# A hybrid decoder layer: its late matrix products computed as eight plain block products in place of seven combined ones

## The chip, the cores and the metric

The kernel runs on one core of one Trainium2 chip, in one launch. The metric is the device time of that launch in microseconds (us). The kernel before takes 2474.23 us, the median of three runs (2469.93 to 2477.15). TensorE does the matrix products. VectorE (DVE), ScalarE (ACT) and GpSimd (POOL) do elementwise work, and every DMA here is issued from the SyncE (SP) queue. Matrix products collect their sums in PSUM, eight banks of 128x512 float32.

## The reference, cut to what matters

SEQ and D_MODEL are 1024, D_FF is 2816, there is one layer and one batch entry.

```
h = rmsnorm(x)
proj = h @ w_in                        # 1024 x 12312: inputs of three mixers, and three gates
y_gla, y_mlstm, y_fox = gla(proj), mlstm(proj), fox(proj)    # each 1024 x 1024
merged = sum over n of (ys[n] @ w_branch[n]) * sigmoid(gates[n] + b_gate[n])
x = x + merged @ w_out
h = rmsnorm(x)
a, g = split(causal_dwconv(h @ w_up))  # 2 x 2816 columns
x = x + (silu(g) * a) @ w_down         # 2816 -> 1024
out = rmsnorm(x)
```

The change touches the three branch products, the product with `w_out` (each 1024x1024x1024) and the product with `w_down` (1024x2816x1024). It leaves the products with `w_in` and `w_up` as they are.

## The kernel before, in words

**Precision.** Operands are float32. Each is split into a high and a low part of type float32r (`split`, L166: ACT casts to get the high part, DVE subtracts to get the low one). A block product is three matmuls: high by high, high by low, low by high. A matmul here has 128x128 weights and a 128x512 moving tile.

**Seven products.** Every large product is cut into 2x2 blocks and computed with seven block products in place of eight (Strassen's scheme in Winograd's form), numbered 1 to 7. For one `Job` (256 output rows by 1024 columns) each of the seven is 4 blocks of depth times 3 matmuls, so 12 matmuls, which the text calls a step. The scheme needs sums of blocks on both sides: of the weights (`prep`, L1157, by POOL at L1168), of the moving side (`combos`, L1035, by POOL or DVE at L1059 to L1069), and of the results (`compute`, L1188, with ACT copies at L1199 and DVE adds at L1090, L1114, L1264, L1276, L1344).

**Order of the work.** `gemms` (L1239) walks one list of steps and prepares the weights of two steps ahead of the one it computes (AHEAD = 2). The list of the first part holds 48 jobs of `w_in` (336 steps), then three branch products of 4 jobs each, then the product with `w_out`, 4 jobs. Beside it `mixers` (L1482) yields small steps of the mLSTM, GLA and FoX mixers in that order. The loop at L1498 takes one mixer step per list step; from list step NX = 110 on it takes a second one in every fourth (RATE = 4). When the mixers are done, the loop of `w_in` runs on alone to its end.

**The moving side.** It lives in seven groups of SBUF of 16 KB per partition (`group`, L152). `put` (L256) splits a 128x512 block into one. When a step is computed, functions hung on it (`after`) call `more`, which loads and prepares the next product's blocks into groups as they come free. The branch products read the mixers' outputs from DRAM (`y_d`), the last reads `w_dn`.

**Merging and the two ends.** `merge_job` (L1079) multiplies a branch result by its gate and adds it to `mg`, two groups; that add is POOL's (L1095). `out_job` (L1101) splits `mg` as its weights and adds the result to x. `row_norm` and `blocks0`, `blocks1` then normalise and transpose the rows for `w_up`. The down product runs in three chunks of depth (8, 8 and 6 blocks); after each step DVE adds the PSUM bank to rows `acc` in SBUF (L1344), and `finish` (L1354) does the final norm of a row and stores it.

**Scheduling.** The instructions of each engine stand in an order that the framework's scheduler fixes at build time from the order of the program text, its own estimate of durations, and free buffers. At run time every engine works its list strictly in that order, except that weight loads of TensorE overlap matmuls.

Of the kernel before, what the change touches and what calls it, by code (L numbers as in the profile page):

```python
# [36 lines left out]
MAP_FF = {1: 3, 2: 4, 5: 0, 6: 1, 3: 2, 7: 5, 4: 6}  # L37
# [4 lines left out]
ROLL_DN = (3, 4, 0, 1, 2, 5, 6)  # L42
DN_CHUNKS = (8, 8, 6)


class Job:
# [3 lines left out]
    def __init__(self, src1, src2, xc, post, name, nk=4, done=None, wide=False, acc=None, load=None, kept=None):  # L50
        self.src, self.xc, self.post, self.name, self.nk = (src1, src2), xc, post, name, nk
        self.done, self.wide, self.acc, self.load = done, wide, acc, load
        self.kept = kept
        self.raw, self.w, self.after = None, {}, {}
        self.second, self.held, self.inplace, self.sum1 = False, None, False, None

# [44 lines left out]
class Kern:  # L101
# [933 lines left out]
    def combos(self, n, block, xc, base, order, ytile, ttile, engs):  # L1035


        nc = self.nc
        ts = [None] * n
        due = []  # L1040

        def load(kh, i, hf):
            t = ytile()
            nc.sync.dma_start(out=t, in_=block(kh, i, hf))
            return t

        for p in order:
            for i in range(n):
                if p == 1:
                    src = load(0, i, 0)  # L1050
                elif p == 2:
                    src = load(1, i, 0)
                elif p == 3:
                    src = load(1, i, 1)
                elif p == 5:
                    b = load(0, i, 0)
                    src = ts[i] = ttile(i)
                    nc.sync.dma_start(out=src, in_=block(0, i, 1))
                    engs[p].tensor_tensor(out=src, in0=src, in1=b, op=ALU.subtract)  # L1059
                elif p == 6:  # L1060
                    b = load(1, i, 1)
                    src = ts[i]
                    engs[p].tensor_tensor(out=src, in0=b, in1=src, op=ALU.subtract)
                elif p == 7:
                    src = load(0, i, 0)
                    engs[p].tensor_tensor(out=src, in0=ts[i], in1=src, op=ALU.subtract)  # L1066
                else:
                    src = load(1, i, 0)
                    engs[p].tensor_tensor(out=src, in0=src, in1=ts[i], op=ALU.subtract)  # L1069
                due.append((p, i, src))  # L1070
                if len(due) > LAG:
                    q, m, t = due.pop(0)
                    self.put(xc, q, m, t, base)
                yield
        while due:
            q, m, t = due.pop(0)
            self.put(xc, q, m, t, base)

    def merge_job(self, env, n, b, p, xc):  # L1079
        nc, a = self.nc, self.a  # L1080

        def post(m, hf, x, y):
            pool, mg = env["late"], env["mg"]
            j = 2 * p + m
            sl = slice(512 * (1 - hf), 512 * (1 - hf) + 512)
            th = pool.tile([P, 512], F32, tag="gth", name="gth", bufs=2)
            nc.sync.dma_start(out=th, in_=self.g_d[8 * b + j][:, sl])
            if y is not None:
                t = x if (m, hf) == (1, 1) else y
                nc.vector.tensor_tensor(out=t, in0=x, in1=y, op=ALU.add)  # L1090
                x = t
            o = mg[j // 4][:, j % 4, sl]
            nc.vector.scalar_tensor_tensor(out=th if n else o, in0=th, scalar=1.0, in1=x, op0=ALU.add, op1=ALU.mult)
            if n:
                nc.gpsimd.tensor_tensor(out=o, in0=o, in1=th, op=ALU.add)  # L1095

        def kept(nm):
            return env["late"].tile([P, 512], F32, tag="s5", name=nm, bufs=4) if nm == "s5" else None
        return Job(a["w_br"][8 * b + 2 * p], a["w_br"][8 * b + 2 * p + 1], xc, post, "br", wide=True, kept=kept)

    def out_job(self, env, p, xc, rows, done):  # L1101

        nc = self.nc

        def load(job):
            mg = env["mg"]
            for i in range(2):
                rows[2 * p + i] = r = self.raw_tile(job, "x2")
                nc.sync.dma_start(out=r, in_=self.a["x"][(2 * p + i) * P:(2 * p + i + 1) * P, :])
            return [mg[kh][:, :, (2 * p + i) * P:(2 * p + i + 1) * P] for i in range(2) for kh in range(2)]  # L1110

        def acc(m, hf, b):
            o = rows[2 * p + m][:, 512 * hf:512 * hf + 512]
            nc.vector.scalar_tensor_tensor(out=o, in0=b, scalar=0.5, in1=o, op0=ALU.mult, op1=ALU.add)  # L1114
        return Job(None, None, xc, None, "wo", wide=True, acc=acc, load=load, done=lambda: done(p))

# [27 lines left out]
    def load_w(self, job):  # L1144
        if job.load is not None:
            job.raw = job.load(job)
            return
# [40 lines left out]
    def compute(self, job, p):  # L1188
        nc, post, acc = self.nc, job.post, job.acc
# [21 lines left out]
        if acc is not None:  # L1211
            if p == 1 or p == 2:
                acc(0, 0, b)
            elif p == 6 or p == 3:
                acc(0, 1, b)
            elif p == 5 or p == 7:
                acc(1, 1, b)
            elif p == 4:
                acc(1, 0, b)
        elif p == 1:  # L1220
# [18 lines left out]
    def gemms(self, seq):  # L1239
        due = []  # L1240
        while True:
            while len(due) <= AHEAD:
                nxt = next(seq, None)
                if nxt is None:
                    break
                job, p = nxt
                if job.raw is None:
                    self.load_w(job)
                self.prep(job, p)
                due.append(nxt)  # L1250
            if not due:
                return
            self.compute(*due.pop(0))
# [84 lines left out]
    def down_job(self, p, k0, nk, acc, wait, xc):  # L1338
        nc = self.nc

        def add(m, hf, b):
            def run():
                o = acc[2 * p + m][:, 512 * hf:512 * hf + 512]
                nc.vector.tensor_tensor(out=o, in0=o, in1=b, op=ALU.add)  # L1344
            if 2 * p + m in acc:
                run()
            else:
                assert hf == 0 and m == 0
                wait.append(run)
        src = [self.f_d[k0:k0 + nk, :, (2 * p + m) * P:(2 * p + m + 1) * P].rearrange("j p t -> p j t")  # L1350
               for m in range(2)]
        return Job(src[0], src[1], xc, None, "dn", nk=nk // 2, wide=True, acc=add)

    def finish(self, pool, x, tt, nfin):  # L1354
        nc = self.nc
        junk = self.swp.tile([P, D], BF16, tag="ws", name="junk", bufs=3)
        sm = pool.tile([P, 3], F32, tag="fsm", name="fsm", bufs=3)
        nc.scalar.activation(junk, x, AF.Square, accum_out=sm[:, 0:1])  # L1358
        self.rsqrt(sm[:, 2:3], sm[:, 0:1], 1.0 / D, sm[:, 1:2], 1)
        nc.vector.scalar_tensor_tensor(out=x, in0=x, scalar=sm[:, 2:3], in1=nfin, op0=ALU.mult, op1=ALU.mult)  # L1360
        nc.sync.dma_start(out=self.a["out"][tt * P:(tt + 1) * P, :], in_=x)
# [4 lines left out]
RATE = 4  # L1366
# [6 lines left out]
def body(tc, stop=None, **a):  # L1373
# [6 lines left out]
    with ExitStack() as ctx:  # L1380
# [10 lines left out]
        V, G = nc.vector, nc.gpsimd  # L1391

        def ytile():
            return env["cmb"].tile([P, 512], F32, tag="yb", name="yb", bufs=4)

        def ttile(i):
            return env["cmb"].tile([P, 512], F32, tag=f"T{i}", name="T")

        def wide(jobs):
            for p, j in enumerate(jobs):  # L1400
                j.second, j.inplace = p > 1, True
            return jobs

        def branch_blocks(b):
            return lambda kh, i, hf: k.y_d[b, 4 * kh + i][:, 512 * (1 - hf):512 * (1 - hf) + 512]

        def dn_blocks(k0, nk):
            return lambda kh, i, hf: a["w_dn"][k0 + kh * (nk // 2) + i][:, 512 * hf:512 * hf + 512]

        def out_blocks(kh, i, hf):  # L1410
            return a["w_out"][4 * kh + i][:, 512 * hf:512 * hf + 512]

        ready = []

        def sequence():
# [4 lines left out]
            for n, b in enumerate(order):  # L1420
                x = {}
                jobs = wide([k.merge_job(env, n, b, p, x) for p in range(4)])
# [363 lines left out]
```

## Time and profile before

| what | value |
|---|---|
| median of 3 runs | 2474.23 us |
| time of the profiled execution | 2473.26 us |
| its span, first to last instruction | 2471.3 us |
| TensorE matmul busy | 2318.3 us (94%), 11035 matmuls |
| VectorE busy | 1899.1 us (77%) |
| ScalarE busy | 1243.4 us (50%) |
| GpSimd busy | 1029.3 us (42%) |
| mean granted clock of TensorE | 0.977 of full speed |

A row of the profile names the line of the kernel, the engine, the operation and what it writes and reads ("x<-yb" writes tile x from tile yb). PE is TensorE. A granted clock of 1.00 is 2.4 GHz; the other level is half of it, so 0.90 over a stretch means that it ran a fifth of it at half speed. Busy time of TensorE is taken from modelled ends, so gaps between the starts of matmuls say more than it does. Stretches of the execution are named by their times from the span's start: the mixers mLSTM (to about 640 us), GLA (to 931) and FoX (to 1368) beside the products with `w_in`; the end of these at 1423.1; branches and `w_out` to 1771.4; the way into `w_up` to 1830.3; `w_up` to 2225.7; down to 2463.3.

### The profile page before, as it was taken

The page shows a single profiled execution, that of the slowest core. Times are in us where ns is not written, and L with a number is a line of the kernel's source. Part 1 is how long each engine was busy: PE and PEld are TensorE (multiplying, and loading weights), DVE is VectorE, ACT ScalarE, POOL GpSimd, SP SyncE. Part 2 cuts the span into 40 slices and gives each one's busy share as a digit, 9 for nine tenths or more (in the row PEclk, how much of TensorE's full clock was granted, in tenths as well). Part 3 has the DMA queues.
Part 4 walks back from the last instruction along what each step waited for, and adds up shares of the span by engine and source line. Part 5 has one row for each costly group of instructions (what it writes and reads, how often), then busy time and mean ns, then how long its engine had stood idle before and what let it go on. Part 6 is the DMA issues. An engine that isn't in the chain of part 4 may idle for free. (4 is left out here: it accounts for less than half of the span.)

```text
span 2471.3 us, 33215 instructions
## 1 busy us (share of the span) xinstructions
PE 2318.3 (94%) x11035; PEld 1905.4 (77%) x11035; DVE 1899.1 (77%) x3124; ACT 1243.4 (50%) x2441; POOL 1029.3 (42%) x972
## 2 busy tenths in 40 slices
PE   6999999988998999999999899888989999988898
PEld 5877778777777888888888787677868888866687
DVE  7687557676576766777776689988788898989986
ACT  5345455555566655555555554342555555553433
POOL 6222144444344443222222453577344443445662
PEclk8999999999999999999999999999999999999999
DMA  3355444554433435343333665553232332244631
GB/s 134 112 172 170 135 139 148 175 175 151 142 126 130 145 120 164 122 132 127 126 128 108 219 204 184 200 180 102 103 101 78 97 99 85 94 141 146 207 120 69
DMA packets 191500, 340.50 MB, mean 138 GB/s; under 512 B 17961, under 2 KB 80201, under 8 KB 190817
## 3 DMA queue, kind: packets, MB, share of 16 engines
q1 hardware_dynamic: 191328, 338.38, 41.9%
q8 instruction: 87, 1.43, 0.2%
q14 instruction: 85, 0.69, 0.1%
HBM read 242.73 MB, written 95.58 MB: 137 GB/s over the span
## 5 line engine op out<-in xcount | busy, mean ns | idle before, releaser
L160 PE MATMUL pg<-x,w6h 128*128 128x512 f32 x776 | 249.2, 401 | 18.1 <-DVE x L168 9.5
L160 PE MATMUL pg<-x,w4h 128*128 128x512 f32 x776 | 248.4, 401 | 13.5 <-DVE u L1264 9.2
L160 PE MATMUL pg<-x,w7h 128*128 128x512 f32 x776 | 247.2, 400 | 5.2 <-ACT u L1199 5.2
L160 PE MATMUL pg<-x,w1h 128*128 128x512 f32 x776 | 244.8, 396 | 3.7 <-ACT w1h L167 3.4
L160 PEld LDWEIGHTS pg<-x,w6h 128*128 128x128 f32 x776 | 146.1, 192 | 52.7 <-DVE x L168 13.2
L1168 POOL TENSOR_TENSOR sum<-up_raw 128x512 f32<-128x512 f32 x44 | 91.0, 2067 | 225.2 <-DMA up_raw<-in_w_up 203.0
L160 PEld LDWEIGHTS pg<-x,w4h 128*128 128x128 f32 x776 | 147.3, 193 | 46.1 <-DVE u L1264 6.4
L160 PEld LDWEIGHTS pg<-x,w7h 128*128 128x128 f32 x776 | 147.3, 193 | 36.3 <-ACT u L1199 6.0
L160 PEld LDWEIGHTS pg<-x,w1h 128*128 128x128 f32 x776 | 146.2, 191 | 34.6 <-ACT w1h L167 3.8
L160 PE MATMUL pg<-x,w7l 128*128 128x512 f32 x388 | 155.3, 400 | 12.8 <-DVE w7l L168 12.8
L160 PE MATMUL pg<-x,w4l 128*128 128x512 f32 x388 | 155.5, 401 | 7.6 <-DVE w4l L168 7.6
L160 PE MATMUL pg<-x,w1l 128*128 128x512 f32 x388 | 153.6, 396 | 6.9 <-DVE w1l L168 6.9
L160 PE MATMUL pg<-x,w6l 128*128 128x512 f32 x388 | 154.3, 398 | 0.1
L168 DVE TENSOR_TENSOR x<-yb,x 128x512 fp32r<-128x512 f32 x135 | 136.4, 1044 | 5.9 <-ACT x L167 4.8
L1313 DVE SCALAR_TENSOR_TENSOR c<-u,cols,c 128x1022 f32<-128x1022 f32 x84 | 126.7, 1508 | 15.5 <-ACT c L1309 15.5
L168 DVE TENSOR_TENSOR w5l<-sum,w5h 128x512 fp32r<-128x512 f32 (+1 forms) x98 | 99.0, 1010 | 37.8 <-ACT w5h L167 32.5
L160 PE MATMUL pa<-x,w3h 128*128 128x512 f32 x392 | 123.3, 394 | 1.7 <-DVE x L168 1.7
L160 PE MATMUL pa<-x,w5h 128*128 128x512 f32 x392 | 124.2, 398 | 0.8 <-DVE acc L1344 0.4
L160 PE MATMUL pg<-x,w5h 128*128 128x512 f32 x384 | 123.7, 402 | 0.9 <-DVE x L168 0.7
L160 PE MATMUL pg<-x,w2h 128*128 128x512 f32 x384 | 122.7, 399 | 1.6 <-POOL x L168 1.6
L160 PE MATMUL pg<-x,w3h 128*128 128x512 f32 x384 | 121.8, 398 | 0.0
L167 ACT CAST w5h<-sum 128x512 fp32r<-128x512 f32 (+1 forms) x98 | 60.2, 615 | 122.0 <-PE pg L160 86.9
(476 smaller groups left out, 6692.2 us busy)
## 6 DMA issues: line engine op xcount, KB each, us to landing
up_raw<-in_w_up SPq DMA_DIRECT2D x44, 512.0 KB, 3.8
yb<-y_d SPq DMA_DIRECT2D x84, 256.0 KB, 3.1
yb<-in_w_dn SPq DMA_DIRECT2D x77, 256.0 KB, 3.5
gate_raw<-in_w_in SPq DMA_DIRECT2D x24, 512.0 KB, 3.7
g_d<-st SPq DMA_DIRECT2D x48, 256.0 KB, 2.1
br_raw<-in_w_br SPq DMA_DIRECT2D x24, 512.0 KB, 4.8
gth<-g_d SPq DMA_DIRECT2D x48, 256.0 KB, 2.9
f_d<-c SPq DMA_DIRECT2D x22, 512.0 KB, 2.9
```

The source lines that it names most:

```text
L160: self.nc.tensor.matmul(out, lhsT=lhsT, rhs=rhs, start=start, stop=stop, skip_group_check=skip)
L167: self.nc.scalar.copy(out=hi, in_=src)
L168: (eng or self.nc.vector).tensor_tensor(out=lo, in0=src, in1=hi.bitcast(F32), op=ALU.subtract)
L1168: self.nc.gpsimd.tensor_tensor(out=t, in0=a, in1=b, op=op)
L1313: nc.vector.scalar_tensor_tensor(out=c[:, s:], in0=u[:, :T - s], scalar=self.col("fw", 44 * tap + m), in1=c[:, s:], op0=ALU.mult, op1=ALU.add)
```

## The change

The four products of the branches and `w_out` and the down product become plain products: eight block products, no block sums. A result stays in two PSUM banks over the whole depth. The products with `w_in` and `w_up` keep the seven.

- `Row` is 128 output rows by 1024 columns in four steps of 12 matmuls. It uses one high weight block for four matmuls (high and low of both halves of the columns), then its low block for two. The gate and merge of a branch read the two banks once per row; the add into `mg` moves from POOL to DVE.
- `Down` computes four rows of 128 at once, in eight banks, over all 22 blocks of depth, twice. It reads the activations `f_d` as weights, 256 KB at a time through two buffers, and keeps 14 of the 22 split blocks of `w_dn` in the seven groups, two to a group; the second half takes the kept ones first.
- `finish` adds the two banks of a row to x, in halves, and does the norm.
- The loads of a moving block are one per block; `yb` has six buffers.
- RATE becomes 10, and in FoX a second mixer step is taken in three of five list steps.
- The group of each step of `w_up` changes (`MAP_FF`); its step 3 is now in group 0, into which the first two blocks of `w_dn` go. Rows of `w_out` are normalised one by one as they get ready.

```diff
-MAP_FF = {1: 3, 2: 4, 5: 0, 6: 1, 3: 2, 7: 5, 4: 6}
+MAP_FF = {1: 1, 2: 2, 5: 3, 6: 4, 3: 0, 7: 5, 4: 6}
-DN_CHUNKS = (8, 8, 6)
+KEEP = 14
-RATE = 4
+RATE = 10
+class Row:
+    def prep(self, k, q):
+        if q % 2 == 0:
+            self.w[q // 2] = k.wsplit(self.raw[q // 2], "wo")
+    def compute(self, k, q):
+        if q == 0:
+            self.banks = (k.pg(), k.pa())
+        for i in range(2):
+            ...
+            x = [self.xc[q][2 * i + hf] for hf in range(2)]
+            first, last = q == 0 and i == 0, q == 3 and i == 1
+            for b, (xh, xl) in zip(self.banks, x):
+                k.mm(b, wh[:, ks], xh, first, False, True)
+                k.mm(b, wh[:, ks], xl, False, False, True)
+            for b, (xh, xl) in zip(self.banks, x):
+                k.mm(b, wl[:, ks], xh, False, last, True)
+        if q == 3:
+            for hf in range(2):
+                self.post(hf, self.banks[hf])
+class Down:
+    def steps(self):
+        n = len(self.order)
+        return [("r", r, 0) for r in range(4)] + [("k", i) for i in range(2, n - 2)] + [("r", r, n - 2) for r in range(4)]
...
 merge_row:
+                th = env["late"].tile([P, 512], F32, tag="gth", name="gth", bufs=4)
+                nc.sync.dma_start(out=th, in_=k.g_d[8 * order[n] + r][:, sl])
+                o = env["mg"][r // 4][:, r % 4, sl]
+                nc.vector.scalar_tensor_tensor(out=th if n else o, in0=th, scalar=1.0, in1=b, op0=ALU.add,
+                                               op1=ALU.mult)
+                if n:
+                    nc.vector.tensor_tensor(out=o, in0=o, in1=th, op=ALU.add)
...
 makes:
+                    m = dn["n"] = dn.get("n", -1) + 1
+                    g = m // 2 % 7
+                    if m % 2 == 0:
+                        dn["t"] = k.group(g, F32R, "xd")
...
+                    raw = k.dnp.tile([P, T], F32, tag="dr", name="dn_raw", bufs=2)
+                    nc.sync.dma_start(out=raw, in_=a["w_dn"][j])
...
 mixers' loop:
-                if n >= NX and n % RATE == RATE - 1:
+                if n % 5 in (0, 2, 4) if fox else n >= NX and n % RATE == RATE - 1:
                     next(mix, None)
...
 finish:
+        x = pool.tile([P, D], F32, tag="xr", name="xr", bufs=3)
+        nc.sync.dma_start(out=x, in_=self.x2_d[tt])
+        for hf, b in enumerate(banks):
+            o = x[:, 512 * hf:512 * hf + 512]
+            nc.vector.tensor_tensor(out=o, in0=b, in1=o, op=ALU.add)
+            nc.scalar.activation(junk[:, 512 * hf:512 * hf + 512], o, AF.Square, accum_out=sm[:, 2 + hf:3 + hf])
```

## Rows read from the trace of the kernel before

**Rows 1.** By stretch: us; PE, PEld, DVE, ACT, POOL busy (count); clock; DMA; GB/s
```profile
331.30:456.50 125.20, 115.86 (x616) 98.56 (x615) 86.60 (x166) 69.69 (x167) 62.72 (x76) 0.99 0.54 171
456.50:640.00 183.50, 167.03 (x902) 143.99 (x901) 125.16 (x259) 100.15 (x248) 77.84 (x93) 0.96 0.49 154
640.00:931.00 291.00, 273.06 (x1410) 226.38 (x1410) 200.72 (x468) 175.90 (x424) 129.42 (x204) 0.98 0.42 136
931.00:1368.00 437.00, 429.91 (x2313) 362.20 (x2312) 304.62 (x831) 234.62 (x492) 117.16 (x183) 1.00 0.39 127
...
1396.90:1423.10 26.20, 19.54 (x74) 15.33 (x73) 19.87 (x21) 13.95 (x24) 15.82 (x11) 0.87 0.67 219
1423.10:1771.40 348.30, 322.11 (x1378) 260.73 (x1377) 306.01 (x373) 149.46 (x268) 190.84 (x125) 0.97 0.50 169
1771.40:1830.30 58.90, 48.23 (x201) 37.27 (x200) 48.70 (x59) 31.18 (x53) 31.84 (x21) 0.91 0.20 70
1830.30:2201.00 370.70, 369.96 (x1633) 306.01 (x1631) 330.73 (x316) 191.23 (x279) 151.24 (x77) 1.00 0.29 94
2201.00:2225.70 24.70, 15.47 (x51) 11.85 (x50) 18.25 (x15) 11.67 (x19) 18.33 (x12) 0.80 0.60 198
2225.70:2340.70 115.00, 95.89 (x386) 75.30 (x385) 108.05 (x118) 43.91 (x75) 67.26 (x42) 0.92 0.57 185
2340.70:2463.30 122.60, 122.60 (x541) 101.09 (x539) 99.81 (x135) 46.13 (x84) 59.52 (x46) 1.00 0.28 91
```

**Rows 2.** Matmuls in order of time at full clock: start us, duration, instruction
```profile
1380.80 0.61 PE L160 MATMUL pg<-x,w2h 128*128 128x512 f32 x2
1381.25 0.39 PE L160 MATMUL pg<-x,w2l 128*128 128x512 f32 x1
1381.48 0.61 PE L160 MATMUL pg<-x,w2h 128*128 128x512 f32 x2
```

**Rows 3.** The same view behind a wait: the clock is at its lower level
```profile
1401.74 1.22 PE L160 MATMUL pg<-x,w7h 128*128 128x512 f32 x2 [4.46 <-ACT u L1199]
...
1403.19 1.05 PE L160 MATMUL pg<-x,w7h 128*128 128x512 f32 x2
1404.04 0.63 PE L160 MATMUL pg<-x,w7l 128*128 128x512 f32 x1
```

**Rows 4.** TensorE's waits, 1423.1 to 1771.4: total us, times, longest
```profile
PE pg L160 <- DVE w7l L168: 7.7, 3, 5.1
```

**Rows 5.** TensorE's waits, 2201.0 to 2225.7
```profile
PE pg L160 <- DVE u L1264: 9.2, 2, 5.9
```

**Rows 6.** VectorE's and GpSimd's groups, 1423.1 to 1771.4: count, busy us, mean ns
```profile
L168 DVE TENSOR_TENSOR x<-yb,x 128x512 fp32r<-128x512 f32 x71 | 70.3, 1028 | 2.4 <-ACT x L167 2.2
L1095 POOL TENSOR_TENSOR mg<-mg,gth 128x512 f32<-128x512 f32 x32 | 52.1, 1627 | 59.1 <-DVE gth L1093 46.3 <-PE pa L160 12.8
...
L168 DVE TENSOR_TENSOR x<-b,x 128x512 fp32r<-128x512 f32 x8 | 5.1, 686 | 0.0
```

**Rows 7.** TensorE's matmuls on tile x alone: us, busy (count), clock, DMA, GB/s
```profile
331.30:456.50 125.20, 86.45 (x362) 0.99 0.54 171
456.50:640.00 183.50, 117.90 (x480) 0.96 0.49 154
640.00:931.00 291.00, 212.18 (x842) 0.98 0.42 136
931.00:1368.00 437.00, 292.41 (x1193) 1.00 0.39 127
```

**Rows 8.** DMA issues: size, median us from issue to landing
```profile
yb<-y_d SPq DMA_DIRECT2D x84, 256.0 KB, 3.1
g_d<-st SPq DMA_DIRECT2D x48, 256.0 KB, 2.1
```

**Rows 9.** The end: VectorE's last instructions in order of time
```profile
2463.45 0.69 DVE L1344 TENSOR_TENSOR acc<-acc,pg 128x512 f32<-128x512 f32 x1
...
2466.34 1.28 DVE L1360 SCALAR_TENSOR_TENSOR acc<-acc,fsm,nfin 128x1024 f32<-128x1024 f32 x1 [0.73 <-POOL fsm L173]
```

More of the change, by code (lines that the diff above doesn't have):

```diff
@@ L1033, in fox @@
                 yield
[L1035 to L1115, printed above, removed]
@@ L1188, in compute @@
     def compute(self, job, p):
[L1189 removed]
+        nc, post = self.nc, job.post
         x = job.xc[p]
@@ L1246, in gemms @@
                 job, p = nxt
-                if job.raw is None:
-                    self.load_w(job)
-                self.prep(job, p)
+                if isinstance(job, (Row, Down)):
+                    if job.raw is None:
+                        job.load(self)
+                    job.prep(self, p)
+                else:
+                    if job.raw is None:
+                        self.load_w(job)
+                    self.prep(job, p)
                 due.append(nxt)
@@ L1252, in gemms @@
                 return
-            self.compute(*due.pop(0))
+            job, p = due.pop(0)
+            if isinstance(job, (Row, Down)):
+                job.compute(self, p)
+            else:
+                self.compute(job, p)
             yield
@@ L1336, in ffn_jobs, with finish @@
             yield Job(a["w_up"][j], a["w_up"][NFF + j], xc, self.to_tiles(dst), "up", done=done, wide=True)
-    def down_job(self, p, k0, nk, acc, wait, xc):
+    def finish(self, pool, tt, banks, nfin):
         nc = self.nc
[L1341 to L1352, printed above, removed]
@@ L1390, in body, with merge_row, load, post @@
         rows = {}
-        V, G = nc.vector, nc.gpsimd
         def ytile():
[L1394 to L1411, printed above, removed]
-        ready = []
+            return env["cmb"].tile([P, 512], F32, tag="yb", name="yb", bufs=6)
+        def merge_row(n, r, x):
+            def load(job):
+                job.second = r % 2 == 1
+                t = k.raw_tile(job, "br_raw")
+                nc.sync.dma_start(out=t, in_=a["w_br"][8 * order[n] + r])
+                return t[:, 0:512], t[:, 512:1024]
+            def post(hf, b):
+                sl = slice(512 * hf, 512 * hf + 512)
+                th = env["late"].tile([P, 512], F32, tag="gth", name="gth", bufs=4)
[5 more added lines that the diff above has]
+                    nc.vector.tensor_tensor(out=o, in0=o, in1=th, op=ALU.add)
+            return Row(x, load, post)
+        ready = []
+        def out_row(r, x):
+            def load(job):
+                job.second = r > 3
+                rows[r] = t = k.raw_tile(job, "x2")
+                nc.sync.dma_start(out=t, in_=a["x"][r * P:(r + 1) * P, :])
+                return [m[:, :, r * P:(r + 1) * P] for m in env["mg"]]
+            def post(hf, b):
+                o = rows[r][:, 512 * hf:512 * hf + 512]
+                nc.vector.scalar_tensor_tensor(out=o, in0=b, scalar=0.5, in1=o, op0=ALU.mult, op1=ALU.add)
+            return Row(x, load, post, lambda: ready.append(r))
         def sequence():
@@ L1573, in pieces @@
-            def pieces():
-                for g in parts:
-                    yield from g
-            gen = pieces()
+            gen = makes()
             made = [0]
-            per = [nk // 2 for _, nk in chunks for _ in range(7)]
             def more(free, most=1):
                 for _ in range(most):
-                    if made[0] < sum(per[:free]) + LAG and next(gen, gen) is not gen:
+                    if made[0] < free and next(gen, gen) is not gen:
                         made[0] += 1
-            after(jobs[-1], 4, lambda: dn.setdefault("up", True))
@@ L1593, in ffn @@
+            used = 0
+            for d in downs:
+                for p in d.steps():
+                    if p[0] == "k":
+                        used += 1
+                    elif p[1] == 3:
+                        used += 2
+                    after(d, p, lambda u=used // 2 * 2: more(KEEP + u))
             yield from products(jobs, LEADS, TAIL)
[L1594 to L1597 removed]
+            for d in downs:
+                for p in d.steps():
+                    yield d, p
```

255 lines of the change are left out of this document (133 added, 122 removed).

## The prediction, made before the changed kernel was run

> **What bounds the kernel now.** I read the view by stretch first, then the matmuls in order of time, then the waits. TensorE bounds nearly everything: in the `w_up` stretch its matmuls are busy 369.96 of 370.70 us with VectorE at 330.73 (89%), and no wait is left [rows 1]. The price of a matmul is the distance between starts: two on the same weights start 1380.80 and the next 1381.25, the third 0.23 later; 0.68 for three, so 0.2267 us each, and 2.72 us for a step of 12 [rows 2]. Behind a wait the clock is at 1.2 GHz and two take 0.85 us [rows 3], so a wait costs its length and about 2.4 us more for the step that follows.
>
> With that price each stretch splits into work and loss, loss being stretch minus matmuls times 0.2267 [rows 1]:
> - End of `w_in`, 26.2 us: 6 steps, 16.3; lost 9.9. One wait of 4.46 us opens it, for ScalarE [rows 3]; I take it that its queue stood at casts of block sums that POOL had not made yet.
> - Branches and `w_out`, 348.3 us: 1378 matmuls, of which 32 are transposes and 2 belong to `w_up`; 1344 by 0.2267 is 304.7. The 32 transposes stay; with 3.6 us put down for them, a guess that stands on both sides and cancels, 40.0 is lost. The waits are for VectorE's low parts [rows 4], and VectorE is busy 306 of 348.
> - Way into `w_up`, 58.9 us: 14 steps, 38.1, and 32 transposes; some 17 lost.
> - End of `w_up`, 24.7 us: 4 steps, 10.9; lost 13.8, of which VectorE's late adds are 9.2 [rows 5].
> - Down, 115.0 and 122.6 us: 924 matmuls, 209.5; lost 28.1, all in the first part (clock 0.92 against 1.00).
> - Mixers: TensorE idle 9.3, 16.5, 17.9 and 7.1 us in the four stretches to 1368.
>
> **The change part by part.** All is summed against the profiled execution's own 2473.26 us, which is 0.97 below the median of the runs.
>
> *Matmuls added.* A 1024-cube takes 8 rows of 48, 384, in place of 4 jobs of 84, 336: +48, four times, +192. Down takes 22 by 8 by 2 by 3, 1056, in place of 924: +132. At 0.2267: +43.5 and +29.9 us, all on the path.
>
> *Branches and `w_out`: lost 40.0, then 3.* What goes: 24 of every 56 splits, the sums, the copies and adds of results. VectorE has left 64 moving blocks, 64 weight blocks, 48 gates, 32 merge adds (POOL's until now, 1.63 each) and 16 adds to x, 224 instructions at 0.69 [rows 6], 154 us of 348 in place of 306. The price 0.69 is the one without POOL at work; with it the same split takes 1.03, and POOL, busy 191 us here, has almost nothing left. The tight places are the four borders between products. The next product's second to fourth groups wait for the current last row's steps to free them; 12 moving blocks, a row's post (4 instructions) and 3 weight blocks, 19 at 0.69, 13.1 us, stand in the 16.3 us from the first group's release to the last group's first use. Behind such a cast on ScalarE wait the casts of weights for the step after next, with 5.4 us in hand; behind its DMA wait on SP the next gate loads, whose four buffers hold two rows. Loads land in 3.1 us [rows 8], and there are 64 in place of 128. For `w_out`, the split of the second half of `mg` waits for the last merge: 0.2+1.4 to the first half, a cast, the subtraction behind two moving blocks, about 5 us, in 5.4. So the four borders fit, barely; I take 3 us in all. Ends: 0, and 28 where each border costs what the opening of the end of `w_in` costs (4.5+2.4). Net +43.5-37.0 = +6.5.
>
> *End of `w_in`: 9.9, then 2.* Its moving blocks come straight from `y_d`, so no cast stands behind POOL. 21 of them enter in 14 steps, 38 us, with 14 weight blocks and some 6 posts: 41 at 0.69 to 1.03, 28 to 42 us; so something may remain. -7.9; ends -9.9 and +4.
>
> *Way into `w_up`: -1.* Norms of three more rows are done early, but the transposes at 10.6 us behind the end of `w_out` did not wait for norms before either; the blocks for steps 5 and 6 set the loss, and they are unchanged. Ends -8 and +5.
>
> *End of `w_up` and start of down: 13.8, then 5.* Here a wait is added. The first two blocks of `w_dn` go to group 0, and step 3 of the last job holds it until 2.7 us before down begins; both raw buffers stand behind, so SP can't load a third block until then. Down then needs two blocks in its first 10.9 us (four row steps) and one per 24 matmuls, 5.4 us, from there on. Four splits at 0.69, two of activations, and the last adds and activation functions of `w_up` are some 7.4 us of VectorE from a start 2.5 us before: 5 late, clock included. The third block, loaded 3.5 us after its buffer is free, is 5 us early. -8.8; ends -13.8 and +6.
>
> *Down: 28.1, then 1.* VectorE has 104 splits at 0.69 and eight norms of 3 us, 96 us of 240 in place of 208; ScalarE less. Nothing else feeds TensorE. Net +29.9-27.1 = +2.8; ends +1.8 and +12.
>
> *The last rows: +1.* Before, 8.0 us pass from the last matmul to the end: an add of 0.69, a square, a scale of 1.28, the store [rows 9]. Now the row's x is loaded at its `finish`, into three buffers; the last row's load waits for the store of the row three earlier. That store leaves some 4.6 us behind that row's last matmul and lands in 2.1 [rows 8], the load takes 3: 9.7, while the last row ends 8.2 behind. Its add is 2 us late; scales in halves give 1 back. Ends -1 and +4.
>
> *Mixers: 0.* The same steps run, so only waits can change. Matmuls on x over 12 give 30, 40, 70 and 99 list steps in the four stretches [rows 7], so 30, 50, 88 and 124 mixer steps (a quarter more from step 110 on). Idle per mixer step is 0.31, 0.33, 0.20 and 0.06 us [rows 1]: the waits go with the steps, hardly with their pace. With the slow clock (0.99 and 0.96) the two mLSTM stretches are 0.35 and 0.48. At one extra in ten, mLSTM and GLA take 125 list steps for 110, and I give them -5. FoX takes 77 for 99. A FoX step is 1.35 us beside a list step's 2.72 (437 over 99 and 124); VectorE, 304.6 us, has some 1.0 per list step (a split and three sevenths of an add, both 0.69), so 1.66 per FoX step, and goes from 70% to 3.66 of 4.88, 75%, below `w_up`'s 89% without a wait; but two of its steps in a row leave less time for a chain through ScalarE and back, so 0.10 for 0.06: +5. The mixers end 7 list steps sooner, and these cost the same alone. Ends: -47 (all idle and slow clock from 456 to 931 gone) and +34 (FoX at mLSTM's 0.33).
>
> *Sum.* +6.5 -7.9 -1 -8.8 +2.8 +1 +0 = -7.4: 2465.9 for the profiled execution, 2467 on the scale of the median.
>
> **A page against the row.** Pairs on the same weights and changes of weights are equally far apart, 0.45 for two and 0.23 [rows 2]. The Trainium skill (TensorE: Matmul & The Clock Gate, "Wait — 56ns, not 53.3ns?") has back-to-back matmuls of 512 columns 215.7 ns apart when warm; the trace has 226.7, and the row decides. By the page the 324 added matmuls would be 69.9 us and not 73.4; it also leaves room for an order of matmuls that runs closer together, which is the last rival.
>
> **The rivals.**
> 1. *FoX pays for its pace, slower.* If two steps in a row make TensorE wait as in mLSTM, 0.33 per step, 124 steps give +34: 2501. It is slower than before from 0.18 per step on. For it: 1.6 FoX steps per list step for 1.25. Against: it already took a quarter of double steps at 0.06.
> 2. *The waits stay: the change doesn't do what it says.* If half the loss in branches, start of down and down comes from elsewhere than sums and results (borders, queues in order), +17, +2 and +13: 2499. For it: the low parts of weights are what TensorE waited for, and they remain. Against: VectorE's load halves there.
> 3. *The calmer mLSTM and GLA give half their idle and slow clock back*, -24: 2443. For it: the clock falls there. Against: idle per step was the same at both paces.
> 4. *The plain order runs closer together.* High weights serve four matmuls in a row; if the distance fell to 512 columns at 2.4 GHz, 213.3 ns, 2592 matmuls would save 35: 2432. Against: rows 2, equal distances.
>
> **How the numbers follow.** Forecast 2467, chance 0.54, by itself 2455 to 2481; rivals 0.14, 0.12, 0.18, 0.02. 2443 to 2496 leaves out half of each rival. About 0.3% (7.4 us) can be told from no change: below 2466.8 is faster, above 2481.6 slower. The forecast lies on that border, so half of it, rivals 3 and 4 make faster 0.47; the rest of it 0.27 same with a little of rival 1; slower 0.25; same 0.28.
>
> **What would show it.** Right: stretches of 48 matmuls in 10.9 us through branches and `w_out`, POOL nearly idle, VectorE splits at 0.69; some 356 us from the first branch matmul to the last of `w_out`; 240 and a start of 5 for down; FoX with under 13 us idle. Wrong: waits longer than 3 us at the borders of products, or for the first blocks of `w_dn`; FoX's idle above 30 us; idle in mLSTM and GLA far from 0.3 and 0.2 per step.

## The result, and the profile after

The changed kernel takes 2437.24 us, the median of four runs (2432.96 to 2440.24), beside 2473.86 of the kernel before on the same chip: ratio 0.9851, 95% interval 0.9828 to 0.9874. It is 1.5% faster. The forecast was 2467, range 2443 to 2496: right in sign, and the time lies below the range.

The profiled execution has a span of 2438.4 us for 2471.3, at a mean granted clock of 0.991 for 0.977. Of its page, the busy time and count of each engine:

```profile
PE 2360.6 (97%) x11359; PEld 1949.6 (80%) x11359; DVE 1599.3 (66%) x2871; ACT 1145.9 (47%) x2268; POOL 676.7 (28%) x752
```

TensorE has 324 matmuls more and is the only engine that works longer; VectorE gave up 300 us and GpSimd 353. The view by stretch, with the columns of [rows 1]; the first line is the start of mLSTM, the next two late mLSTM and GLA, the fourth FoX, then the end of `w_in`, branches and `w_out`, the way into `w_up`, `w_up`, its end, down, and the last rows:

```profile
332.00:459.50 127.50, 117.53 (x618) 100.01 (x616) 87.51 (x167) 69.97 (x167) 62.89 (x76) 0.97 0.53 167
459.50:656.00 196.50, 185.53 (x1000) 158.94 (x999) 136.54 (x270) 108.49 (x262) 83.47 (x101) 0.99 0.49 158
656.00:956.00 300.00, 294.28 (x1517) 244.94 (x1516) 205.87 (x480) 182.84 (x438) 131.60 (x209) 0.99 0.43 142
956.00:1332.50 376.50, 370.75 (x2033) 309.27 (x2032) 278.97 (x796) 211.05 (x451) 101.95 (x171) 1.00 0.39 127
...
1368.00:1395.50 27.50, 27.46 (x121) 22.45 (x120) 19.56 (x29) 19.60 (x35) 4.25 (x3) 1.00 0.81 275
1395.50:1747.60 352.10, 352.10 (x1569) 291.62 (x1568) 143.24 (x231) 80.77 (x138) 7.65 (x10) 1.00 0.35 120
1747.60:1806.60 59.00, 48.41 (x201) 37.35 (x200) 47.25 (x56) 30.09 (x50) 29.12 (x18) 0.91 0.18 61
1806.60:2164.00 357.40, 356.66 (x1574) 295.11 (x1573) 318.88 (x302) 182.38 (x263) 143.84 (x74) 1.00 0.25 83
2164.00:2188.50 24.50, 24.50 (x110) 20.30 (x109) 17.16 (x22) 12.71 (x22) 4.26 (x3) 1.00 0.12 43
2188.50:2427.90 239.40, 239.40 (x1057) 198.09 (x1056) 92.32 (x146) 70.42 (x131) 3.29 (x6) 1.00 0.41 139
2427.90:2438.40 10.50, 0.17 (x1) 0.00 (x0) 4.95 (x11) 1.33 (x4) 1.10 (x2) 0.67 0.51 194
```

The reader is to compare three things with [rows 1]. From 1395.5 to 1747.6 TensorE is busy all the time at full clock, where it was 322.11 of 348.30 at 0.97; so it is at the end of `w_in`, at the end of `w_up` and in down. The last rows take 2.4 us longer. And FoX ends at 1332.5 where it ended at 1368, although GLA takes longer and FoX begins some 20 us later: the branches begin 27.6 us sooner (1395.5 for 1423.1), and the end of `w_in` had under 10 us to give. The rest, 18 us, is what the forecast had at nothing.

The matmuls on tile x in mLSTM, GLA and FoX (us, busy and count, clock, DMA, GB/s), as in [rows 7], give the list steps by which to divide, 48, 79 and 76:

```profile
459.50:656.00 196.50, 137.61 (x577) 0.99 0.49 158
656.00:956.00 300.00, 234.95 (x949) 0.99 0.43 142
956.00:1332.50 376.50, 231.70 (x914) 1.00 0.39 127
```

With 1.1 mixer steps per list step, TensorE's idle time per mixer step is 10.97/53 = 0.21 us in mLSTM and 5.72/87 = 0.07 in GLA. The forecast read 0.33 and 0.20 before, and assumed that they stay. In FoX, at 1.6 per list step, it is 5.75/122 = 0.05, for 0.06 at 1.25.

### The profile page after: what moved, and what is told of

Same layout as the page of the kernel before. It is cut to its first block, busy times and chain, and to the rows that moved or that the text cites. A ratio compares the mean times of both kernels' runs of the same rounds, so it can differ in the third digit from the quotient of the medians.

```text
span 2438.4 us, 32792 instructions
## 1 busy us (share of the span) xinstructions
PE 2360.6 (97%) x11359; PEld 1949.6 (80%) x11359; DVE 1599.3 (66%) x2871; ACT 1145.9 (47%) x2268; POOL 676.7 (28%) x752
## 4 chain that ended last, share of the span: by engine, by line
PE 79%; DVE 8%; DMA 4%; ACT 3%; POOL 3%; issue 2%; SPq 0%; DVEq 0%; POOLq 0%; ACTq 0%
PE pg L248 49%; PE pa L248 28%; PE pa L252 3%; DMA mw<-mw_d 1%; DVE x L256 1%; POOL sum L1171 1%; POOL sm L261 1%; DVE w3l L256 0%; DVE st L1279 0%; DMA fv<-fv_d 0%; DMA fvo_raw<-in_w_in 0%; POOL mw L634 0%; DVE t L368 0%; DVE c L1316 0%; DVE e L805 0%
## 5 line engine op out<-in xcount | busy, mean ns | idle before, releaser
L248 PE MATMUL pg<-x,w6h 128*128 128x512 f32 x560 | 182.6, 404 | 11.8 <-DVE x L256 10.6
L248 PE MATMUL pg<-x,w4h 128*128 128x512 f32 x560 | 175.5, 394 | 1.3 <-DVE xm L1267 0.8
L248 PE MATMUL pg<-x,w1h 128*128 128x512 f32 x560 | 176.4, 395 | 0.0
L248 PE MATMUL pg<-x,w7h 128*128 128x512 f32 x560 | 175.2, 393 | 0.7 <-ACT u L1202 0.7
L248 PE MATMUL pg<-x,woh 128*128 128x512 f32 x512 | 158.1, 390 | 0.0
L248 PE MATMUL pa<-x,woh 128*128 128x512 f32 x512 | 157.7, 389 | 0.0
L248 PEld LDWEIGHTS pg<-x,w4h 128*128 128x128 f32 x560 | 103.7, 188 | 24.2 <-DVE xm L1267 1.2
L248 PEld LDWEIGHTS pg<-x,w7h 128*128 128x128 f32 x560 | 102.9, 188 | 22.0 <-ACT u L1202 1.2
L248 PEld LDWEIGHTS pa<-x,woh 128*128 128x128 f32 x512 | 96.1, 188 | 20.0
L248 PEld LDWEIGHTS pg<-x,woh 128*128 128x128 f32 x512 | 96.1, 188 | 19.8
L248 PE MATMUL pg<-x,w7l 128*128 128x512 f32 x280 | 109.4, 391 | 0.0
```

The lines of the kernel that those rows point to most:

```text
L248: self.nc.tensor.matmul(out, lhsT=lhsT, rhs=rhs, start=start, stop=stop, skip_group_check=skip)
```

## The experiments

Ratios are to the kernel before on the same chip. "Loss" is the sum of what the gaps between the starts of matmuls have beyond the usual gap of that kind of matmul; unlike idle time it holds the time at the lower clock too. "Seconds" are second mixer steps. Start: first branch matmul; then the lengths, in us, of branches and `w_out`, of `w_up` up to the first matmul of down, of down, and from the last matmul to the end. The ratios are of medians; the other columns are of one profiled execution each.

| kernel | ratio | seconds in late mLSTM, GLA | loss there | seconds in FoX | loss there | start | branches, `w_out` | `w_up` | down | end |
|---|---|---|---|---|---|---|---|---|---|---|
| before | 1 | 28 | 53.8 | 24 | 15.4 | 1423.1 | 348.0 | 395.4 | 237.6 | 8.1 |
| changed | 0.9851 | 13 | 29.6 | 46 | 18.5 | 1395.5 | 352.1 | 381.8 | 239.4 | 10.5 |
| e1 | 0.9936 | 28 | 52.8 | 24 | 15.3 | 1416.7 | 352.1 | 381.9 | 239.4 | 10.5 |
| e2 | 0.9960 | 28 | 53.0 | 45 | 22.7 | 1422.4 | 352.1 | 381.9 | 239.4 | 10.5 |
| e3 | 0.9903 | 13 | 32.0 | 46 | 17.1 | 1405.2 | 347.8 | 396.8 | 237.4 | 8.1 |
| e4 | 0.9839 | 0 | 22.8 | 45 | 22.7 | 1394.4 | 352.1 | 381.9 | 239.4 | 10.5 |
| e5 | 0.9926 | 28 | 51.0 | 24 | 17.9 | 1415.6 | 352.1 | 381.9 | 239.4 | 10.5 |
| e6 | 0.9888 | 13 | 41.4 | 45 | 18.1 | 1406.5 | 352.1 | 381.9 | 239.4 | 10.5 |
| e7 | 0.9985 | 28 | 59.1 | 24 | 16.7 | 1421.9 | 352.1 | 398.1 | 234.9 | 8.4 |
| e8 | 0.9984 | 28 | 55.6 | 24 | 14.5 | 1423.9 | 348.2 | 387.0 | 239.4 | 10.5 |
| e9 | 0.9768 | 28 | 53.1 | 24 | 15.2 | 1415.9 | 325.3 | 388.4 | 220.2 | 7.9 |
| e10 | 0.9856 | 28 | 56.1 | 24 | 16.5 | 1428.5 | 325.5 | 392.9 | 223.9 | 8.4 |
| e11 | 0.9853 | 0 | 22.1 | 45 | 25.3 | 1397.0 | 352.1 | 381.9 | 239.4 | 8.8 |
| e12 | 1.0009 | 47 | 59.6 | 46 | 27.0 | 1431.8 | 352.1 | 381.8 | 239.4 | 10.5 |

**e1: the changed kernel at the pace of before.**

```diff
-RATE = 10
+RATE = 4
-                if n % 5 in (0, 2, 4) if fox else n >= NX and n % RATE == RATE - 1:
+                if n >= NX and n % RATE == RATE - 1:
```

> The changed kernel with the mixers' old pace everywhere (from list step 110 on a second mixer step in every fourth list step, also in FoX). Theory P (the new pace takes waits out of mLSTM and GLA, where double steps crowd a chain): the first branch matmul moves from 1395.5 back to about 1413, idle of TensorE in GLA returns from 5.7 to about 18 us, the time is about 2437+18 = 2455. Rival Q (the order in which the scheduler happens to lay the instructions, not the pace): some other time between 2432 and 2445. Rival R (FoX's quicker pace is what saves): also about 2455, so this run alone does not tell P from R.

Measured: 2460.99, ratio 0.9936 [0.992, 0.9952]. More than half of the gain is gone, all of it before the branches. Theory P has its place and size right there (branches at 1416.7 for about 1413, 17.9 us idle in GLA for about 18) and its total 6 us too low; rival Q is out. GLA, with the columns of [rows 1], has its idle time and its clock of 0.98 back, 17.86/89 = 0.20 us idle per mixer step as in the kernel before:

```profile
644.00:937.00 293.00, 275.14 (x1422) 228.32 (x1421) 203.03 (x468) 176.55 (x426) 131.82 (x205) 0.98 0.42 137
```

**e2: the old pace up to FoX, the new one in FoX.** The first line of e1's diff alone.

> The changed kernel with the old pace in mLSTM and GLA (every fourth list step) and the new one in FoX (three of five). Theory P: the waits of GLA return and FoX stays under 8 us idle, so about 2455 as with the old pace everywhere. Rival R: about 2437, as the changed kernel. Rival Q: neither, 2432 to 2460.

Measured: 2467.11, 0.996 [0.9947, 0.9974]. Rival R is out, but theory P's total is 12 us too low too, and FoX is idle 9.2 us for the "under 8". FoX's quick pace saves nothing by itself; it loses 7 us more than in e1 and ends 54 us sooner, time that plain `w_in` steps then fill. It may make room for a slow pace before it; no run has the slow pace without it. The changed kernel differs from e2 in `RATE` alone, and is 1.1% faster.

**e3: the kernel before, at the new pace.** The reverse of e1's diff, in the kernel before.

> The kernel before with the new pace alone (every tenth list step, three of five in FoX); seven products everywhere. Theory P: 2474-18 = 2456, idle in GLA about 6 us, the loss at the end of w_in (9.9 us), in the branches (40) and in down (28) as before. Rival Q: within 5 us of 2474 or anything else; the pace would then not be worth the same in both kernels.

Measured: 2454.49, 0.9903 [0.9886, 0.992]: 24 us (interval 20 to 28) of a change of two lines, without any of the plain products; of the two profiled executions, whose loss the table shows, this one is 17 us shorter. Theory P holds, with 6.3 us idle in GLA for the "about 6". With e1's 0.64% it adds up to 1.6%, and both together measured 1.5%. The end of `w_in` still loses 9.3 us.

**e4: no second steps before FoX.**

```diff
-                if n % 5 in (0, 2, 4) if fox else n >= NX and n % RATE == RATE - 1:
+                if fox and n % 5 in (0, 2, 4):
```

> The changed kernel with no second mixer step at all before FoX, then three of five. Theory P, if waits go with the double steps: a few us less idle in mLSTM and GLA, 2430 to 2437. If only the crowding of one in four mattered: the same within 3 us. Rival Q: anything in 2430 to 2450.

Measured: 2437.98, 0.9839 [0.9824, 0.9853], 1 us above theory P's range. Late mLSTM and GLA lose 7 us less, FoX 4 more; the intervals of e4 and of the changed kernel overlap, so the gain of calming has run out. Its rows of late mLSTM and GLA give 8.88/54 = 0.16 and 4.54/86 = 0.05 us idle per mixer step:

```profile
460.60:671.30 210.70, 201.82 (x1077) 172.53 (x1076) 147.14 (x282) 113.47 (x274) 90.57 (x102) 0.99 0.51 159
671.30:987.00 315.70, 311.16 (x1602) 258.95 (x1601) 215.34 (x489) 190.16 (x450) 138.93 (x215) 1.00 0.44 141
```

**e5 and e6: is it the PSUM banks?** e5 is e1 with GLA's transposed keys put into the bank of its scores; e6 is the changed kernel with one of the four `pa` banks held all through GLA.

```diff
-                pt = self.pa()[:, 0:P]
+                pt = ps[:, 256:256 + P]
```

```diff
+        hold = self.pa()
+        nc.vector.memset(hold[:, 0:8], 0.0)
...
+        nc.vector.tensor_copy(out=S[:, 0:8], in_=hold[:, 0:8])
```

> The changed kernel with the old pace everywhere, and GLA's transposed keys put into the PSUM bank of its scores (one bank of the four named pa less per chunk). Theory B (what the double steps wait for is a bank of pa: the waits named are all for matmuls into pa, behind an instruction that empties one): lost time in GLA falls from 27.6 us (old pace) to 18 or less, so 10 us or more below the old pace's 0.9936 of the kernel before, 0.9895 or less. Rival C (the chain through the state, its split and the queues of VectorE and ScalarE): within 3 us of the old pace, 0.992 to 0.995.

> The changed kernel with one of the four pa banks kept from use all through GLA (a few columns written at its start and read at its end). Theory B: lost time in GLA goes from 13 us to 30 or more, time up by 15 us or more against the changed kernel's 0.985 of the kernel before, so 0.991 or more. Rival C: up by 5 us at most, 0.987 or less.

Measured: e5 2460.67, 0.9926 [0.9897, 0.9955], and GLA's loss 25.1 for e1's 27.6; e6 2449.37, 0.9888 [0.9865, 0.9911], and GLA's loss 23.1 for 13.2. A bank less hurts, a use less hardly helps: e5 comes out as rival C said, e6 between the two, and neither theory is decided. TensorE's waits in GLA (who waits for whom: us in total, times, longest) are in the kernel before (640 to 931):

```profile
PE pa L164 <- DVE S L805: 7.1, 3, 3.5
PE pa L164 <- ACT o L810: 4.8, 4, 2.0
...
PE pa L164 <- DVE ktl L168: 1.6, 1, 1.6
```

in the changed kernel (656 to 956):

```profile
PE pa L252 <- ACT o L898: 4.5, 5, 2.4
PE pa L252 <- DMA vr<-gv_d: 0.9, 1, 0.9
```

and in e6 (657 to 968):

```profile
PE pa L252 <- ACT o L898: 8.1, 6, 2.6
PE pa L252 <- DMA vr<-gv_d: 2.3, 2, 1.8
PE pa L252 <- DVE S L893: 1.2, 2, 0.7
```

The slower pace takes away three waits of up to 3.5 us for VectorE's update of the state S. They are there at the old pace in both kernels (7.0 us in e1) and gone at the new pace in both; with no second steps (e4) there is one of 1.8 us. With a bank held (e6) the wait for S is 1.2 us, and the one for ScalarE's copy `o` grows from 4.5 to 8.1. In the kernel's text the update and the copy each read a `pa` bank, so both waits are waits until a bank is read out: theory B names what is waited for, theory C would be why it comes late, and the two don't exclude each other. Nor is the wait for S the price of pace as such. With 1.5 mixer steps per list step (e12 below, 626.9 to 891.7) it is 0.3 us, and other waits stand in its place:

```profile
PE pa L252 <- ACT o L898: 9.4, 6, 2.2
PE pa L248 <- DVE Sl L256: 3.1, 2, 2.5
...
PE pa L252 <- DVE S L891: 0.3, 1, 0.3
```

**e7 and e8: the plain products one at a time, in the kernel before.** e7 has the branches and `w_out` as in the change, and its `MAP_FF`; e8 has the down product with the old `MAP_FF`, so blocks of `w_dn` come into other groups, and sooner, than in the change.

```diff
-                jobs = wide([k.merge_job(env, n, b, p, x) for p in range(4)])
+                make = (lambda r, x, n=n: merge_row(n, r, x)) if n < 3 else out_row
+                gemm.append(([make(r, x) for r in range(8)], x))
...
```

```diff
-                ds = [k.down_job(p, k0, nk, acc, wait, x) for p in range(4)]
+        downs = [Down(0, first, xs, dn_done), Down(1, again, xs, dn_done)]
...
```

> The kernel before with plain products in the branches and for w_out only; seven products for down, the mixers' old pace. If the parts add up as the traces divide them: end of w_in -9.9, branches and w_out +3.6, so -6 us, 0.9975 of the kernel before. By the prediction's own terms -2.4, 0.999. If the two plain parts help each other (shared groups of SBUF), it comes out slower than 0.999.

> The kernel before with plain products for down only (blocks of w_dn into the groups in the order in which w_up frees them); the rest as before. If the parts add up: end of w_up -13.6, down +1.8, last rows +2.5, so -9 us, 0.996 of the kernel before. By the prediction's terms -5, 0.998. If the parts help each other, slower than 0.999.

Measured: e7 2474.46, 0.9985 [0.9972, 0.9997]; e8 2474.49, 0.9984 [0.997, 0.9999]. Each part gives 3 to 4 us. e7's interval holds both numbers expected of it; e8 is near the prediction's terms and 6 us short of what the traces promised. The two add up to 0.3%, while e1, which has both, gains 0.64%: together they are worth more than one by one, and the two lines of the pace, 1%, are worth more than either. By the traces e8 falls short at the end of `w_up`, which loses 5 us where the changed kernel loses nothing. TensorE waits 3.4 us there for a copy `u` of ScalarE (at 2199.65), which stands behind a cast of `w_dn` that waited for its DMA and one that waited for a sum of GpSimd:

```profile
2194.76 1.14 ACT L257 CAST xd<-dn_raw 128x512 fp32r<-128x512 f32 x2 [2.39 <-DMA dn_raw<-in_w_dn]
2198.09 0.62 ACT L257 CAST w3h<-sum 128x512 fp32r<-128x512 f32 x1 [2.19 <-POOL sum L1258]
```

In the changed kernel no cast waits for a DMA there, and the first block of `w_dn` is cast only at 2186.33; that this is what saves the 5 us was not tried by itself. e7 shows the end of `w_in` mended by the branches' plain blocks alone (its loss in the 17 steps behind FoX is 0.1 for 9.7), but also a mixers' loss 5 us above before at the same pace. I take this for the scatter of the loss column, since each edit has the instruction lists laid anew; no run shows that it is.

**e9 and e10: what had made the loss of the seven products?** The kernel before without the block sums of the moving side (e9), and without GpSimd's sums of the weights (e10).

```diff
-                    b = load(0, i, 0)
-                    src = ts[i] = ttile(i)
-                    nc.sync.dma_start(out=src, in_=block(0, i, 1))
-                    engs[p].tensor_tensor(out=src, in0=src, in1=b, op=ALU.subtract)
+                    src = load(0, i, 1)
...
```

```diff
         def comb(t, a, b, op, nm):
+            if job.inplace or job.name == "dn":
+                return a
```

> The kernel before, with the block sums of the moving side left out in the branches, w_out and down (a block is loaded and split where a sum of two blocks was; the output is therefore not the reference's, the number of matmuls and splits is the same). Theory M (TensorE's lost time there, 10 us at the end of w_in, 40 in branches and w_out, 14 + 28 at the end of w_up and in down, comes from casts that stand behind these sums): the end of w_in loses under 1 us, branches and w_out take about 325 for 348, the start of down and down lose some 15 in all; about 2420 in all. Rival W (it comes from the sums of the weights on POOL, whose results are split late): end of w_in goes too, but branches stay at 343 to 348 and down at 232 to 238; about 2460.

> The kernel before, with POOL's sums of the weights left out in the branches, w_out and down (one summand is split in place of the sum; output not the reference's, matmuls and splits unchanged). Theory M: the end of w_in keeps its 10 us, branches and w_out fall by at most 10, down by at most 8: about 2455. Rival W: branches and w_out fall to about 318, down to about 218: about 2422, with the end of w_in still at 10. If neither alone moves its stretch by 10 us, the copies and adds of results on VectorE are what is left.

Measured: e9 2418.81, 0.9768 [0.9737, 0.9798]; e10 2440.81, 0.9856 [0.9825, 0.9887]. Theory M is right on e9's total and branches (1.8 us idle are left at the end of `w_in`, where it said under 1), and theory W nearer on e10's branches and down: neither is the whole. In both kernels branches and `w_out` fall to 325, which leaves 17 us of loss for 40, so leaving out either kind of sum gives back more than half of it, and the two shares overlap. I read it as a loss of load: VectorE's busy time there falls from 306 us to 268 and 265, in e10 with 372 instructions for 373 [rows 1], so by shorter ones alone. But the casts no longer stand behind a sum either, and no run parts the two, nor takes the copies and adds of results alone. The end of `w_in` is separate: most of it hangs on the moving sums, with 1.8 us idle without them and 6.4 without the weights' for 6.7 before. First e9, then e10, columns of [rows 1]:

```profile
1389.70:1415.90 26.20, 24.42 (x106) 19.55 (x105) 17.10 (x24) 16.61 (x30) 7.26 (x6) 1.00 0.82 273
1415.90:1741.20 325.30, 313.55 (x1377) 257.31 (x1376) 267.70 (x341) 148.62 (x265) 149.44 (x102) 0.99 0.52 170
```

```profile
1402.30:1428.50 26.20, 19.76 (x73) 15.77 (x74) 18.03 (x21) 13.76 (x25) 11.06 (x7) 0.87 0.66 218
1428.50:1754.00 325.50, 313.55 (x1378) 256.80 (x1377) 264.88 (x372) 148.79 (x267) 95.72 (x64) 0.99 0.55 180
```

**e11: three edits towards a faster version.** e4's pace, e5's shared bank, and the tile of the last norms in four buffers.

```diff
-        x = pool.tile([P, D], F32, tag="xr", name="xr", bufs=3)
+        x = pool.tile([P, D], F32, tag="xr", name="xr", bufs=4)
```

> The changed kernel with three edits: no second mixer steps before FoX; GLA's transposed keys in the bank of its scores; four buffers for the x rows of the last norms in place of three. Theory C (pace sets the mixers' idle, the last row's x waits for its buffer): start of branches 1393 to 1395 for 1395.5, the tail 8.2 to 8.5 for 10.5; 2433 to 2435 in all, ratio to before 0.982 to 0.984. Rival: the tail is the chain of the norm itself and stays at 10.5, and the mixers' loss stays at 45 to 48 us: 2437, ratio 0.985.

Measured: 2439.08, 0.9853 [0.9826, 0.988], no better than the changed kernel: theory C is right on the end alone. The end takes 8.8 us for 10.5, so 1.7 of the 2.4 us lost there were the buffer. The mixers give nothing more: GLA loses 10.6 with the shared bank and 9.3 without it (e4), and FoX 25.3.

**e12: a second step in every other list step before FoX.**

```diff
-RATE = 10
+RATE = 2
```

> The changed kernel with a second mixer step in every other list step before FoX (RATE = 2 in place of 10). The gaps between matmuls of late mLSTM and GLA beyond their usual distance are 53.8 us with 28 second steps (before), 29.6 with 13 (changed), 22.8 with none: 1.1 us for each. Theory P (the price hangs on the second steps): with 47 of them 22.8 + 52 = 74 us, 44 more than in the changed kernel; 2481 or more in all, ratio to before about 1.002. Rival S (the forecast's view, the idle hangs on the mixer steps and hardly on pace): 140 mixer steps at the 0.34 us of before make 48 us, 2455; at the 0.21 of the changed kernel 29 us, 2437 (ratio 0.985 to 0.992).

Measured: 2477.4, 1.0009 [0.9998, 1.0019]. One number turned the whole gain into nothing, 4 us below the least that theory P allowed, and by another sum: late mLSTM and GLA lose 59.6 us, between S's 48 and P's 74, and FoX 27.0 for 18.5. The rows of late mLSTM and GLA:

```profile
457.50:626.90 169.40, 154.33 (x829) 131.98 (x828) 118.40 (x251) 96.06 (x240) 73.01 (x93) 0.95 0.50 158
626.90:891.70 264.80, 244.30 (x1281) 200.80 (x1281) 182.99 (x452) 163.53 (x406) 114.95 (x198) 0.99 0.44 139
```

At 33.8 and 59.3 list steps of 1.5 mixer steps that is 0.30 and 0.23 us idle per mixer step. In order of pace (1, 1.1, 1.25, 1.5) mLSTM has 0.16, 0.21, 0.33, 0.30 and GLA 0.05, 0.07, 0.20, 0.23. Between 1.25 and 1.5 idle goes about with the steps, as the forecast had it; the largest fall lies between 1.25 and 1.1. The price of a second step isn't the constant 1.1 us of theory P: 29.6 to 53.8 us over 15 of them is 1.6, the next 19 cost 0.3 each.

## Why the prediction was wrong

The terms against the measured stages of the profiled executions (span 2471.3 to 2438.4):

| step | forecast | measured |
|---|---|---|
| mixers | 0 | -18.1 |
| end of `w_in` | -7.9 | -9.5 |
| branches and `w_out` | +6.5 | +4.1 |
| way into `w_up` | -1 | 0 |
| end of `w_up`, start of down | -8.8 | -13.6 |
| down | +2.8 | +1.8 |
| last rows | +1 | +2.4 |
| sum | -7.4 | -32.9 |

**The step that failed** is "Mixers: 0", and in it the sentence "the waits go with the steps, hardly with their pace". The comparison under it, 0.31 us idle per mixer step from 331 to 456 at one step per list step and 0.33 after that at 1.25, was one of two phases and not of two paces. In the changed kernel the first stretch, still at one step per list step, is as before (9.97 us idle in 127.5), while the second falls from 0.33 to 0.21, and at pace 1 late mLSTM has 0.16 (e4) where the beginning has 0.31. So the beginning of mLSTM is dearer at the same pace, and this hid the price of pace behind it. The prediction's own next figure spoke against it: with the slow clock counted, the two stretches cost 0.35 and 0.48 per step, and the forecast made next to nothing of it. The forecast gave mLSTM and GLA -5 us and FoX +5; the losses changed by -24.2 (list step 110 on) and +3.1, and by +2 in the first stretch. e1 and e3 show it from both sides, 21 and 24 us for the pace alone (by the traces 21 and 17).

Rival 3 named this mechanism, with -24 us, and had a chance of 0.18. Its sum of -31.4 us comes within 1.5 of the measured -32.9, in part by luck: it gave the mixers 6 us too much, and the other terms together were 7.4 too dear. (Its 2443 is 6 us above the median; on the scale of the profiled execution, the slowest of the four runs, it is 2442 for 2440.24.) The other terms:

- *Borders of products*, 3 us: they lost nothing. TensorE is busy 352.10 of 352.10. The 0.69 per split without GpSimd held, and the 13.1 us of VectorE work fitted into the 16.3 us.
- *Start of down*, 5 us: it lost nothing. The wait that the change adds exists. The first casts of `w_dn` stand at 2186.33 and VectorE's four splits at 2187.07, 1.4 us before down begins at 2188.5; the loads of the third and fourth block follow at 2188.39. But the splits went ahead of the adds and activation functions that the forecast had put before them, so the first block was ready at 2188.4 and nothing was late. In order of time (start us, duration, instruction):

```profile
2186.33 2.18 ACT L255 CAST xd<-dn_raw 128x512 fp32r<-128x512 f32 x4
2186.47 0.68 DVE L1267 TENSOR_TENSOR u<-u,pa 128x512 f32<-128x512 f32 x1
2187.07 2.49 DVE L256 TENSOR_TENSOR xd<-dn_raw,xd 128x512 fp32r<-128x512 f32 x4
2188.39 1.54 SPq L1567 DMA_DIRECT2D dn_raw<-in_w_dn  x2
```

- *End of `w_in`*, 2 us left: 0.2 are left. Its cause was read rightly. In the kernel before, the copy `u` that TensorE waits for at 1401.74 [rows 3] stands on ScalarE behind a cast that waited for a block sum of GpSimd, and without these sums (e9) most of the loss is gone:

```profile
1400.58 0.62 ACT L167 CAST x<-T 128x512 fp32r<-128x512 f32 x1 [2.72 <-POOL T L1059]
1401.11 0.58 ACT L1199 COPY u<-pg 128x512 f32<-128x512 f32 x1
```

- *Last rows*, +1: +2.4. The mechanism was the one forecast, the row's x in three buffers; the add was later. It is at 2430.60, 2.7 us behind TensorE's end, where it had been 0.15 behind [rows 9], and there are two:

```profile
2426.53 0.33 SPq L1344 DMA_DIRECT2D xr<-x_d  x1
```

```profile
2430.60 0.69 DVE L1349 TENSOR_TENSOR xr<-pg,xr 128x512 f32<-128x512 f32 x1
2431.20 0.68 DVE L1349 TENSOR_TENSOR xr<-pa,xr 128x512 f32<-128x512 f32 x1
```

**What was right.** The price of 0.2267 us per matmul: down is 1056 matmuls in 239.40 us, and all of its loss is gone. So the order of the matmuls saved nothing, and rival 4 is out. (By the 215.7 ns that the Trainium skill gives, in TensorE: Matmul & The Clock Gate, "Wait — 56ns, not 53.3ns?", an estimate for down is 227.8 us; the trace disagrees here as it did before the change.) FoX bears 1.6 steps per list step, so rival 1 is out, and its own bound (under 13 us idle) is met with 5.75; rival 2 (waits that stay) is out in all three stretches. That the seven products' extra work made the 40 us lost in branches and `w_out` holds, for the sums by e9 and e10; the share of the results' copies and adds is not shown. The plain products buy them back with 43.5 us of matmuls.

**What stays open.** Why idle in mLSTM and GLA falls most between 1.25 and 1.1 mixer steps per list step. `RATE` sets how many second steps there are and also at which steps of a mixer they fall, and runs with 2, 4, 10 and none don't tell number from place. That the instructions which empty the banks of `pa` come late is seen in the waits, and e6 shows that banks matter; why they are late no run took apart.

## What to carry to other kernels

When work is interleaved by a fixed ratio, the ratio has a price of its own: read it from the same phase at two paces, or try it alone first, since it is one line. Two stretches of one trace at different paces are also two different phases. Price by stage what a cheaper algorithm costs the helping engines: here seven products for eight saved 324 matmuls and lost all of that again to waits for sums, casts and results.

## What the runs showed of the hardware

VectorE's time for one and the same subtraction depends on whether GpSimd works beside it. The groups of `x<-yb,x` in branches and `w_out` (count, busy us, mean ns, idle before), e9 with GpSimd busy 149 of 325 us, e10 with 96, and the changed kernel with 8:

```profile
L168 DVE TENSOR_TENSOR x<-yb,x 128x512 fp32r<-128x512 f32 x96 | 92.0, 1000 | 2.3 <-ACT x L167 2.2
```

```profile
L168 DVE TENSOR_TENSOR x<-yb,x 128x512 fp32r<-128x512 f32 x71 | 50.5, 752 | 3.1 <-ACT x L167 2.7
```

```profile
L256 DVE TENSOR_TENSOR x<-yb,x 128x512 fp32r<-128x512 f32 x47 | 30.3, 689 | 8.7 <-ACT x L255 8.5
```

With 1028 ns at 191 us of GpSimd before [rows 6], the mean falls with GpSimd's share. It is a mean of two kinds. Of the instructions of this group in branches and `w_out` of the kernel before, the 43 that start while GpSimd is idle take 675 to 693 ns. Of the 27 that start while a GpSimd instruction runs, all but one end 545 to 553 ns after that instruction ends, and take up to 1791 ns; e9 and e10 show the same. So such a subtraction is held until GpSimd's instruction is over. One pair of rows, where GpSimd ends at 1596.75 and the subtraction at 1597.28:

```profile
1595.01 1.74 POOL L1168 TENSOR_TENSOR sum<-br_raw 128x512 f32<-128x512 f32 x1
```

```profile
1595.51 1.77 DVE L168 TENSOR_TENSOR x<-yb,x 128x512 fp32r<-128x512 f32 x1
```

The Trainium skill (GPSIMD Engine Reference, section 1, Specifications) says that GpSimd's access to SBUF is shared with VectorE and contends with VectorE instructions of two SBUF inputs, which this one is. The four means and the two kinds agree with it.
